# An opening of eight groups of weight columns in a decoder layer on one core, with one load of forget weights and an earlier copy of c

## The chip, the core and the metric

One NeuronCore of a Trainium2 chip runs the whole layer in one launch. The metric is the device time of one execution in microseconds. TensorE (PE in the profile) multiplies into eight PSUM banks; VectorE (DVE), ScalarE (ACT) and GpSimd (POOL) do the rest; SyncE (SP) only issues loads.

## What is computed

One decoder layer on 512 positions of 1024 channels, in float32. Two attention branches read the same modulated input u; one combined projection gives queries, keys and values of both, the forget logits of eight heads and two sets of 1024 gates:

```python
mod = c @ w_ada + b_ada
sh1, sc1, gt1, sh2, sc2, gt2 = jnp.split(mod, 6)
u = x * (1.0 + sc1) + sh1
proj = u @ w_in     # fox q,k,v | forget logits | stick-breaking q,k,v | gates A | gates B
log_f = log_sigmoid(f_a + b_forget)
y_fox = softmax(q k^T / 8 + cumsum(log_f)_t - cumsum(log_f)_s, causal) v
y_sb = stick_breaking(q k^T / 8) v
merged = sigmoid(g_a) * (y_fox @ w_fox_proj) + sigmoid(g_b) * (y_sb @ w_sb_proj)
x = layer_norm(alpha * x + (1 + gt1) * (merged @ w_o))
...                 # then a gated MLP with a causal convolution, and a second layer norm
```

## The kernel before

Every product is made of three in a reduced float32: an operand is split into a high part h (a rounded copy, by ScalarE) and a low part l (the difference, by VectorE), and h x h, l x h and h x l are summed in a PSUM bank. One such product has 128 x 128 weights and 512 positions.

**The opening** (lines 222 to 395) runs over the eight tiles j of 128 input channels. `first_load` (line 250) issues the loads of a tile on SP's queue: the two rows `wa` of w_ada for shift and scale, the row `r` of the first weight columns (`w1`, W1C = 904 columns: 128 for the first pair's queries, 128 for its keys, NG = 5 gate groups of 128 for the stick-breaking branch, and 8 forget columns), and x. Tile 0's row is loaded in two parts, columns 0 to 383 and 384 to 903. The small bias of the forget logits is loaded behind tile 6.

c is spread over all partitions by eight select products into banks 6 and 7 (line 234), among warm-up products (`heat`) that keep TensorE working. For tile 0, `first_acc` (line 272) sums w_ada times c on VectorE straight out of these two banks, half of c at a time; then `first_mod` has ScalarE copy the two banks into `cbc` (line 339), from which all later sums read. `bcols` holds the biases; ScalarE adds 1.0 to some of its columns (line 131). For the other tiles `mod_col` (line 243) makes a sum of 1024 and an addition, once for shift and once for scale.

`first_split` (line 294) has ScalarE copy a row to `wh`; `first_mod` (line 312) makes u of the tile, its high and low part, and the low part of the weights. For tile 0 VectorE makes u's high part itself (line 331) while ScalarE makes the full u. `first_pad` (line 304) makes the rest of tile 0's low part and copies the 8 forget columns to `fw`. `first_mm` (line 363) issues the products of a tile: 7 groups x 3 = 21, each group into a bank of its own (grp[0] to grp[6]), accumulated over the eight tiles. Groups 0 to 4 of a tile come first, then the next tile's `first_mod`, then groups 5 and 6. For tile 0 the high products of groups 0 to 2 come ahead of the rest. At tile 7, `forget_mm` (line 356) puts the eight forget products between groups: they write bank 7, which c had before.

**The stream.** Everything else of the projections is a list of work (`stream`, lines 707 to 816): the other pairs' queries and keys, the values, the remaining gates of the stick-breaking branch (`gb`, groups 5 to 7), and later the gates of the other branch and the output projections. Each piece has a weight load of 512 KB (`add_item`), split by ScalarE and VectorE. `add_ada` puts in a further row of w_ada, which costs VectorE a sum and TensorE nothing.

**The heads.** From line 855 on, sixteen heads run, eight stick-breaking ones first. Each head's scores (`stage_a`), transposes (`stage_b`) and products with the values (`stage_c`) are interleaved with products from the stream: `fill(n)` issues n of them. `FILL` (line 48) has the three amounts for each of the first eight heads and of the last eight. Behind the opening, `gate_after` (lines 840 and 847) takes the sigmoid of the gate banks.

Only SP's order is written by hand; on the other engines a scheduler orders the instructions by their dependencies, held in places by `issue_after`. `paced` makes one instruction wait for another.

Of the kernel before, what the change touches and what calls it, by code (L numbers as in the profile page):

```python
# [8 lines left out]
F32 = mybir.dt.float32  # L9
# [3 lines left out]
ALU = mybir.AluOpType  # L13
# [12 lines left out]
NH = 8  # L26
ALPHA = 2.0 ** 0.25
EPS = 1e-5
NEG = -1.0e30
W1C = 904  # L30
NG = 5
PAIRS = [(1, p) for p in range(4)] + [(0, p) for p in range(4)]
# [14 lines left out]
CUT = 5  # L47
FILL = (15, 18, 18), (11, 11, 11)


@with_exitstack
def layer_kernel(ctx: ExitStack, tc: tile.TileContext, out, xT, x, c8, wa0, wa1, bcol, w1, wct, wv, bf,
                 wp, wo, lncol, lnrow, wup, cwb, wdp):
# [30 lines left out]
    def const(shape, dt, s):  # L84
        return cons.tile(shape, dt, name=s, tag=s)
# [43 lines left out]
    g = G.tensor_copy(crow[0:KT], c8s)  # L129
    for q in (slice(1, 2), slice(3, 6)):  # L130
        S.activation(bcols[:, q, :], bcols[:, q, :], AF.Copy, bias=1.0)
    mska = preset([P, 512], F32, "mska")
# [7 lines left out]
    G.tensor_copy(dg[:, 384:512], ident)  # L140
    bfs = const([NH, 1], F32, "bfs")
    modc = const([P, 4, KT], F32, "modc")
# [82 lines left out]

    fw = early.tile([P, KT, NH], F32, name="fw", tag="fw")
    us = []
    def heat(n):
# [3 lines left out]
    for k in range(KT):  # L232
        o = grp[6 + k // 4][:, k % 4 * P : (k % 4 + 1) * P]
        m = PE.matmul(o, sel[:, k : k + 1].broadcast_to([P, P]), ctop, start=True, stop=True)
    with tc.issue_after(m.ins):
        heat(WARM[1])
# [6 lines left out]
    def mod_col(w, col, wt):  # L243
        mod_sum(w, col, wt, slice(0, D), 0)
        b, o = bcols[:, w, col : col + 1], modc[:, w, col : col + 1]
        return V.tensor_tensor(o, modr[:, w, col, 0:1], b, ALU.add)

    x0 = early.tile([P, 512], F32, name="x0", tag="x0")

    def first_load(j):  # L250
        wa = [early.tile([P, D], F32, name=nm("wa"), tag="wa", bufs=5) for _ in range(2)]
        r = stg.tile([P, 1024], F32, name=nm("raw"), tag="raw", bufs=LOADS)
        xt = z(F32, "xt")
        if j == 0:
            for e in range(2):
                nc.sync.dma_start(wa[e], wa0[j, e])
            nc.sync.dma_start(r[:, 0:384], w1[j][:, 0:384])
            nc.sync.dma_start(x0, xT[j * P : (j + 1) * P, :])
            nc.sync.dma_start(r[:, 384:W1C], w1[j][:, 384:W1C])
        else:  # L260
            nc.sync.dma_start(wa[0], wa0[j, 0])
            if j == 1:
                nc.sync.dma_start(wa[1], wa0[j, 1])
            nc.sync.dma_start(r[:, 0:W1C], w1[j])
            if j > 1:
                nc.sync.dma_start(wa[1], wa0[j, 1])
            nc.sync.dma_start(xt, xT[j * P : (j + 1) * P, :])
            if j == 6:
                nc.sync.dma_start(bfs, bf)
        pend[j] = [wa, xt, r]  # L270

    def first_acc(j):
        wa = pend[j][0]
        if j == 0:
            s = state["chl"]
            for e in range(2):
                for q in range(2):
                    c = slice(q * 512, (q + 1) * 512)
                    with tc.issue_after(s.ins):
                        s = mod_sum(q, j, wa[e], c, e, grp[6 + e])  # L280
                    if e or q:
                        for m in heat(WARM[2] + e * q):
                            paced(m, s)
                    if e and not q:
                        with tc.issue_after(s.ins):
                            s = V.tensor_tensor(bcols[:, 0:2, j], bcols[:, 0:2, j], modr[:, 0:2, j, 0], ALU.add)
            with tc.issue_after(s.ins):
                state["modc"] = V.tensor_tensor(modc[:, 0:2, j], modr[:, 0:2, j, 1], bcols[:, 0:2, j], ALU.add)
        else:
            if j == 1:  # L290
                mod_col(0, j, wa[0])
            state["modc"] = mod_col(1, j, wa[1])

    def first_split(j):
        r = pend[j][2]
        h = stg.tile([P, 1024], F32R, name=nm("wh"), tag="wh", bufs=WBUFS)
        l = stg.tile([P, 1024], F32R, name=nm("wl"), tag="wl", bufs=WBUFS)
        if j:
            hi_of(h[:, 0:W1C], r[:, 0:W1C])
        else:  # L300
            state["h"] = S.activation(h[:, 0:384], r[:, 0:384], AF.Copy)
        pend[j][2:] = [h, l, r]

    def first_pad(j):
        h, l, r = pend[j][2:]
        if j == 0:
            c = slice(384, W1C)
            state["after"] = lo_of(l[:, c], r[:, c], h[:, c])
        f = slice(W1C - NH, W1C)
        hi_of(fw[:, j, :], r[:, f])  # L310

    def first_mod(j):
# [15 lines left out]
        else:  # L328
            h, l, r = pend[j][2:]
            with tc.issue_after(state["modc"].ins):  # L330
                ts = V.tensor_scalar(a, x0, sc, sh, ALU.mult, ALU.add)
            with tc.issue_after(state["h"].ins):
                u = S.activation(xt, x0, AF.Identity, bias=sh, scale=sc)
            c = slice(384, W1C)
            with tc.issue_after(u.ins):
                u = S.activation(h[:, c], r[:, c], AF.Copy)
            for e in range(2):
                with tc.issue_after(u.ins):
                    u = state["u"] = S.activation(cbc[:, e * 512 : (e + 1) * 512], grp[6 + e], AF.Copy)
            with tc.issue_after(ts.ins):  # L340
# [22 lines left out]
    def first_mm(j, gs):  # L363
        ops = [(g, n, m) for g in gs for n, m in enumerate(first_ops(j, g))]
        if j < KT - 1:
            rank = (0, 2, 4, 1, 3, 5)
            ops.sort(key=(lambda o: rank[o[1]] + 3 * (o[0] > 2) if o[0] < 5 else o[1]) if j == 0 else lambda o: o[1])
        for g, n, (w, u) in ops:
            m = PE.matmul(grp[g], w, u, start=j == 0 and n == 0, stop=j == KT - 1 and n == 2)  # L369
        return m  # L370
# [3 lines left out]
    first_split(0)  # L374
    first_acc(0)
    first_mod(0)
    for j in range(KT):
# [11 lines left out]
        if j < KT - 1:  # L389
            first_mm(j, range(5, 7))  # L390
        else:
            forget_mm(first_mm(j, (2, 0, 1)))
            first_mm(j, range(3, 7))

# [261 lines left out]

    sg, ma, wps = {}, {}, {}

    def gate_after(br, j):
# [108 lines left out]
    add_pair(3)  # L768
    add_gate(1, gb.pop(0))
    add_pair(4)  # L770
# [74 lines left out]
    stage_a(1, 0)  # L845
    for j in range(1, NG):
        gate_after(1, j)(grp[2 + j])
# [524 lines left out]
def _pack(inputs):  # L1372
# [16 lines left out]
    def col(kind, n):  # L1389
        if kind in ("sb", "fox"):  # L1390
# [4 lines left out]
    first = [w_in[:, s : s + P] for s in [col("q", 0), col("k", 0)] + [col("sb", j) for j in range(NG)]]  # L1395
    cols = np.concatenate(first + [w_in[:, 1536:1544]], axis=1)
    r["w1"] = c(cols.reshape(KT, P, W1C))
# [3 lines left out]
    r["wct"] = c(np.stack([w_in[:, s : s + P].reshape(KT, P, P).transpose(1, 0, 2).reshape(P, D) for s in starts]))  # L1401
    r["bf"] = c(a["b_forget"].reshape(NH, 1))
    wpj = np.stack([a["w_fox_proj"], a["w_sb_proj"]]).reshape(2, 4, P, 4, 2, P)
# [13 lines left out]

_NAMES = ["xT", "x", "c8", "wa0", "wa1", "bcol", "w1", "wct", "wv", "bf", "wp", "wo", "lncol", "lnrow",
          "wup", "cwb", "wdp"]
# [19 lines left out]
```

## Time and profile before

| | us |
|---|---|
| median of 3 runs | 734.72 |
| lowest, highest | 734.35, 735.94 |
| the profiled execution | 734.0 |
| its span, first to last instruction | 732.2 |
| TensorE busy | 722.6 (99%) |
| VectorE busy | 601.1 (82%) |
| ScalarE busy | 391.7 (53%) |
| GpSimd busy | 88.1 (12%) |

The profile has one execution. In a timeline row stand the start, the time, the engine, the line of the kernel, the operation, what is written and read, its shape, how many instructions are merged into the row, and in brackets how long the engine was idle before and what ended that. Matmuls overlap: the start of the next tells what one costs.

### The profile page before, as it was taken

To read this page: it belongs to the slowest core of one execution; us is meant where nothing else is said; L and a number is where in the kernel's file an instruction comes from. 1 tells how busy PE (TensorE), PEld (TensorE's weight loads), DVE (VectorE), ACT (ScalarE), POOL (GpSimd) and SP (SyncE) were. 2 spreads that over 40 slices of the span, in tenths; PEclk is the share of its full clock that TensorE was granted. 3 is DMA by queue.
4 is the path that set the end of the run, shared out by engine and by line. 5 is a ranking of instruction groups with operands and counts; after the bars stand their busy time and mean duration, and the time that the engine had idled before them with its cause. 6 is when DMAs were issued, how large, how long until landed. Compare 5 with 4: busy or idle time off the path is not lost.

```text
span 732.2 us, 9844 instructions
## 1 busy us (share of the span) xinstructions
PE 722.6 (99%) x3444; PEld 602.3 (82%) x3444; DVE 601.1 (82%) x1041; ACT 391.7 (53%) x684; POOL 88.1 (12%) x142
## 2 busy tenths in 40 slices
PE   8999999999999999999999999999999999999996
PEld 5878888888888888888889888888888888888885
DVE  7978799778898886873697999978887787679996
ACT  5576466686885754442056553444453544347550
POOL 1045224352010000000000001000011010000010
PEclk9999999999999999999999999999999999999999
DMA  9953535423332241632075688577699777646733
GB/s 354 404 208 126 175 116 196 149 88 115 118 116 100 75 170 60 228 124 86 1 259 143 205 250 250 162 249 227 200 349 252 210 239 209 203 161 227 223 89 92
DMA packets 45490, 131.96 MB, mean 180 GB/s; under 512 B 6168, under 2 KB 7200, under 8 KB 45440
## 3 DMA queue, kind: packets, MB, share of 16 engines
q1 hardware_dynamic: 38176, 112.61, 44.6%
q0 software_dynamic: 4224, 10.30, 7.0%
q10 hardware_dynamic: 3040, 8.42, 3.1%
q8 instruction: 27, 0.44, 0.2%
q14 instruction: 23, 0.19, 0.1%
HBM read 118.39 MB, written 12.85 MB: 179 GB/s over the span
## 4 chain that ended last, share of the span: by engine, by line
PE 97%; DMA 1%; DVE 1%; ACT 0%; issue 0%; DVEq 0%
PE ps L152 19%; PE ps L154 19%; PE ps L153 19%; PE ps L1152 5%; PE ps L1153 5%; PE ps L1154 5%; PE ps L369 5%; PE ps L613 3%; PE ps L595 2%; PE ps L521 2%; PE ps L523 2%; PE ps L522 2%; PE ps L944 2%; PE ps L945 2%; PE ps L943 2%; PE ps L547 1%
## 5 line engine op out<-in xcount | busy, mean ns | idle before, releaser
L217 ACT ACTIVATE wh<-raw 128x1024 fp32r<-128x1024 f32 (+1 forms) x105 | 109.1, 1041 | 105.0 <-PE ps L153 47.2
L94 DVE TENSOR_TENSOR wl<-raw,wh 128x1024 fp32r<-128x1024 f32 (+2 forms) x114 | 137.2, 1204 | 30.6 <-ACT wh L217 29.5
L152 PE MATMUL ps<-u2h,wh 128*128 128x512 f32 (+1 forms) x376 | 141.3, 376 | 0.0
L153 PE MATMUL ps<-u2l,wh 128*128 128x512 f32 (+1 forms) x376 | 141.2, 375 | 0.0
L154 PE MATMUL ps<-u2h,wl 128*128 128x512 f32 (+1 forms) x376 | 141.2, 375 | 0.0
L153 PEld LDWEIGHTS ps<-u2l,wh 128*128 128x128 f32 x376 | 70.8, 188 | 12.8
L154 PEld LDWEIGHTS ps<-u2h,wl 128*128 128x128 f32 x376 | 70.8, 188 | 12.8
L152 PEld LDWEIGHTS ps<-u2h,wh 128*128 128x128 f32 x376 | 70.8, 188 | 12.7
L152 PE MATMUL ps<-uh,wh 128*128 128x512 f32 x200 | 79.5, 397 | 0.0
L154 PE MATMUL ps<-uh,wl 128*128 128x512 f32 x200 | 78.1, 391 | 0.0
L153 PE MATMUL ps<-ul,wh 128*128 128x512 f32 x200 | 77.9, 390 | 0.0
L1205 ACT ACTIVATE cv<-ps,cw 128x512 f32<-128x512 f32 x44 | 34.0, 774 | 48.1 <-PE ps L154 40.9
L1206 DVE SCALAR_TENSOR_TENSOR cv<-ps,cw,cv 128x511 f32<-128x511 f32 x44 | 32.8, 746 | 23.0 <-ACT cv L1205 23.0
L154 PEld LDWEIGHTS ps<-uh,wl 128*128 128x128 f32 x200 | 37.5, 188 | 8.3
L153 PEld LDWEIGHTS ps<-ul,wh 128*128 128x128 f32 x200 | 37.6, 188 | 7.4
L152 PEld LDWEIGHTS ps<-uh,wh 128*128 128x128 f32 x200 | 37.5, 188 | 7.4
L240 DVE SCALAR_TENSOR_TENSOR raw<-raw,cbc 128x1024 f32<-128x1024 f32 x32 | 39.6, 1240 | 0.0
L575 POOL TENSOR_TENSOR pt<-pt,om 128x127 f32<-128x127 f32 (+3 forms) x32 | 38.6, 1217 | 1.4 <-DVE om L574 1.3
L181 POOL DMA_DIRECT2D raw<-in_wdp x10 | 8.9, 886 | 244.6 <-DMA raw<-in_wdp 228.1
L1207 DVE SCALAR_TENSOR_TENSOR cv<-ps,cw,cv 128x510 f32<-128x510 f32 x44 | 32.8, 744 | 0.4
L574 DVE TENSOR_TENSOR_SCAN om<-om,dg 128x127 f32<-128x127 f32 (+3 forms) x32 | 28.9, 962 | 3.8 <-ACT om L569 3.8
L1218 ACT ACTIVATE cv<-cv 128x512 f32<-128x512 f32 x21 | 13.3, 631 | 32.0 <-DVE cv L1207 32.0
(246 smaller groups left out, 1551.8 us busy)
## 6 DMA issues: line engine op xcount, KB each, us to landing
raw<-in_wup SPq DMA_DIRECT2D x44, 512.0 KB, 5.0
raw<-in_wa SPq DMA_DIRECT2D x32, 512.0 KB, 3.6
raw<-in_wct SPq DMA_DIRECT2D x25, 512.0 KB, 4.6
raw<-in_wdp SPq DMA_DIRECT2D x20, 512.0 KB, 5.2
wa<-in_wa SPq DMA_DIRECT2D x16, 512.0 KB, 8.7
raw<-in_wdp SPq DMA_DIRECT2D x22, 256.0 KB, 4.7
raw<-t SPq DMA_DIRECT2D x22, 256.0 KB, 4.7
raw<-in_wdp POOLq DMA_DIRECT2D x10, 512.0 KB, 7.7
```

The costliest lines, as they stand in the source:

```text
L94: state["read"] = V.tensor_tensor(o, i, fl(hi), ALU.subtract)
L152: PE.matmul(ps, wh, ah, start=first, stop=False)
L153: PE.matmul(ps, wh, al, start=False, stop=False)
L154: return PE.matmul(ps, wl, ah, start=False, stop=last)
L217: state["hi"] = S.activation(h[:, 0:cols], r[:, 0:cols], AF.Copy)
L240: state["read"] = V.scalar_tensor_tensor(wt[:, c], wt[:, c], 1.0, cbc[:, c] if by is None else by, ALU.mult, ALU.mult, accum_out=o)
L369: m = PE.matmul(grp[g], w, u, start=j == 0 and n == 0, stop=j == KT - 1 and n == 2)
L575: G.tensor_tensor(pt[b][:, s : e - 1], pt[b][:, s : e - 1], om[:, s + 1 : e], ALU.mult)
L1152: PE.matmul(ps, ah, bh, start=first, stop=False, skip_group_check=onto)
L1153: PE.matmul(ps, ah, bl, start=False, stop=False, skip_group_check=onto)
L1154: return PE.matmul(ps, al, bh, start=False, stop=last, skip_group_check=onto)
L1205: tap = S.activation(t, ps, AF.Identity, bias=cw[:, n, 3:4], scale=cw[:, n, 2:3])
```

## The change

W1C becomes 1024 and NG 6: the row of the opening holds six gate groups and no forget columns, and each tile has eight groups, 24 products, into all eight banks. The forget weights come in one load `fwt` of [128, 65] floats, with the bias in its last column, behind tile 6. At tile 7 group 7 is first, its sigmoid is taken at once, and the forget products come behind groups 2 and 3. In the stream the gate behind pair 3 goes (its w_ada row stays), and FILL's first triple is 15, 17, 16.

For tile 0, ScalarE copies bank 7 right behind the select products and bank 6 once VectorE has made its second sum, instead of both behind the weights. VectorE makes u's high part in two halves of 256 positions, and the high products of groups 0 and 1 are issued in halves, first halves first. One product of zeros goes into each of banks 0 and 1 as a warm-up product and opens them, so that the halves can accumulate; four warm-up products among the sums become three. `mod_col` makes one addition for shift and scale together.

```diff
-W1C = 904
-NG = 5
+W1C = 1024
+NG = 6
...
-FILL = (15, 18, 18), (11, 11, 11)
+FILL = (15, 17, 16), (11, 11, 11)
...
-    for q in (slice(1, 2), slice(3, 6)):
-        S.activation(bcols[:, q, :], bcols[:, q, :], AF.Copy, bias=1.0)
...
-    bfs = const([NH, 1], F32, "bfs")
+    fwt = const([P, KT * NH + 1], F32, "fwt")
+    fw = fwt[:, 0 : KT * NH].rearrange("p (k h) -> p k h", h=NH)
+    bfs = fwt[0:NH, KT * NH : KT * NH + 1]
...
         m = PE.matmul(o, sel[:, k : k + 1].broadcast_to([P, P]), ctop, start=True, stop=True)
+    s = S.activation(cbc[:, 512:1024], grp[7], AF.Copy)
+    for q in (slice(1, 2), slice(3, 6)):
+        with tc.issue_after(s.ins):
+            s = S.activation(bcols[:, q, :], bcols[:, q, :], AF.Copy, bias=1.0)
+    state["bcols"] = s
...
-        mod_sum(w, col, wt, slice(0, D), 0)
-        b, o = bcols[:, w, col : col + 1], modc[:, w, col : col + 1]
-        return V.tensor_tensor(o, modr[:, w, col, 0:1], b, ALU.add)
+        s = mod_sum(w, col, wt, slice(0, D), 0)
+        if w:
+            s = V.tensor_tensor(modc[:, 0:2, col], modr[:, 0:2, col, 0], bcols[:, 0:2, col], ALU.add)
+        return s
...
             if j == 6:
-                nc.sync.dma_start(bfs, bf)
+                nc.sync.dma_start(fwt, fwb)
...
                         s = mod_sum(q, j, wa[e], c, e, grp[6 + e])
+                    if q and not e:
+                        with tc.issue_after(state["bcols"].ins):
+                            state["copy"] = S.activation(cbc[:, 0:512], grp[6], AF.Copy)
                     if e or q:
-                        for m in heat(WARM[2] + e * q):
-                            paced(m, s)
+                        m = PE.matmul(grp[q if e else 5], warm[:, 0:P], warm, start=True, stop=not e)
+                        paced(m, s)
...
-            state["h"] = S.activation(h[:, 0:384], r[:, 0:384], AF.Copy)
+            first_acc(0)
+            with tc.issue_after(state["copy"].ins):
+                state["h"] = S.activation(h[:, 0:384], r[:, 0:384], AF.Copy)
...
-        f = slice(W1C - NH, W1C)
-        hi_of(fw[:, j, :], r[:, f])
...
-            with tc.issue_after(state["modc"].ins):
-                ts = V.tensor_scalar(a, x0, sc, sh, ALU.mult, ALU.add)
+            ts = state["modc"]
+            for c in (slice(0, H), slice(H, T)):
+                with tc.issue_after(ts.ins):
+                    ts = V.tensor_scalar(a[:, c], x0[:, c], sc, sh, ALU.mult, ALU.add)
...
-            for e in range(2):
-                with tc.issue_after(u.ins):
-                    u = state["u"] = S.activation(cbc[:, e * 512 : (e + 1) * 512], grp[6 + e], AF.Copy)
+            state["u"] = u
...
-        for g, n, (w, u) in ops:
-            m = PE.matmul(grp[g], w, u, start=j == 0 and n == 0, stop=j == KT - 1 and n == 2)
+        split = 2 if ops[0][0] == 0 and j == 0 else 0
+        for c in (slice(0, H), slice(H, T)):
+            for g, n, (w, u) in ops[0:split]:
+                m = PE.matmul(grp[g][:, c], w, u[:, c], start=False, stop=False)
+        for g, n, (w, u) in ops[split:]:
+            m = PE.matmul(grp[g], w, u, start=j == 0 and n == 0 and g > 1, stop=j == KT - 1 and n == 2)
...
         if j < KT - 1:
-            first_mm(j, range(5, 7))
+            first_mm(j, range(5, 8))
         else:
-            forget_mm(first_mm(j, (2, 0, 1)))
-            first_mm(j, range(3, 7))
+            first_mm(j, (7, 0, 1))
+            sg[(1, NG - 1)] = z(F32, "sg")
+            S.activation(sg[(1, NG - 1)], grp[7], AF.Sigmoid)
+            forget_mm(first_mm(j, (2, 3)))
+            first_mm(j, range(4, 7))
...
     add_pair(3)
-    add_gate(1, gb.pop(0))
+    add_ada()
...
-    for j in range(1, NG):
+    for j in range(1, NG - 1):
         gate_after(1, j)(grp[2 + j])
...
```

## Rows read from the trace of the kernel before

**Rows 1.** Busy us of the engines, share of the span, instructions (page).

```profile
PE 722.6 (99%) x3444; PEld 602.3 (82%) x3444; DVE 601.1 (82%) x1041; ACT 391.7 (53%) x684; POOL 88.1 (12%) x142
```

**Rows 2.** TensorE's waits, whole run: who, for whom, us in total, times, longest.

```profile
PE ps L369 <- DVE uh L331: 0.3, 1, 0.3
PE ps L369 <- ACT uh L317: 0.2, 1, 0.2
```

**Rows 3.** Chain that ended last, 0 to 20 us: start, us, what.

```profile
4.12 7.34 DMA raw<-in_w
...
11.48 0.69 ACT wh L91
...
12.35 0.81 ACT uh L317
```

**Rows 4.** Timeline of TensorE, 0 to 62 us.

```profile
3.30 1.05 PE L234 MATMUL ps<-crow,sel 128*128 128x128 bf16 x8
4.15 1.81 PE L229 MATMUL ps<-warm 128*128 128x512 bf16 x4
...
7.03 0.60 PE L229 MATMUL ps<-warm 128*128 128x512 bf16 x2 [0.29 <-DVE wa L240]
7.93 0.93 PE L369 MATMUL ps<-uh,wh 128*128 128x512 f32 x3 [0.29 <-DVE uh L331]
...
12.34 0.61 PE L369 MATMUL ps<-ul,wh 128*128 128x512 f32 x2
13.20 1.43 PE L369 MATMUL ps<-uh,wh 128*128 128x512 f32 x5 [0.25 <-ACT uh L317]
...
23.06 1.30 PE L369 MATMUL ps<-uh,wh 128*128 128x512 f32 x5
...
42.10 0.39 PE L369 MATMUL ps<-uh,wh 128*128 128x512 f32 x1
...
49.00 0.39 PE L152 MATMUL ps<-uh,wh 128*128 128x512 f32 x1
...
52.30 0.28 PE L546 MATMUL ps<-m,s 128*128 128x256 f32 x1
52.41 0.28 PE L547 MATMUL ps<-m,s 128*128 128x256 f32 x1
```

**Rows 5.** Timeline of all engines, 0 to 20 us.

```profile
5.60 0.69 DVE L240 SCALAR_TENSOR_TENSOR wa<-wa,ps 128x512 f32<-128x512 f32 x1
...
5.72 0.32 ACT L131 ACTIVATE bcols<-bcols 128x8 f32<-128x8 f32 x2 [2.46 <-DMA bcols<-in_bcol]
...
6.23 0.52 ACT L301 ACTIVATE wh<-raw 128x384 fp32r<-128x384 f32 x1 [0.19 <-DMA raw<-in_w]
...
7.01 0.16 DVE L288 TENSOR_TENSOR modc<-modr,bcols 128x2 f32<-128x2 f32 x1
...
7.24 0.55 DVE L331 TENSOR_SCALAR uh<-x,modc 128x512 fp32r<-128x512 f32 x1
7.70 0.55 DVE L94 TENSOR_TENSOR wl<-raw,wh 128x384 fp32r<-128x384 f32 x1
...
8.47 1.06 ACT L339 ACTIVATE cbc<-ps 128x512 f32<-128x512 f32 x2
...
11.48 0.96 ACT L91 ACTIVATE wh<-raw 128x904 fp32r<-128x904 f32 x1 [1.86 <-DMA raw<-in_w]
```

**Rows 6.** DMA issues (KB each, us to landing); windows (last: clock, DMA share, GB/s).

```profile
raw<-in_w SPq DMA_DIRECT2D x7, 452.0 KB, 8.0
...
10.00:11.00 1.00, 1.00 (x7) 0.80 (x6) 1.00 (x3) 0.00 (x0) 0.00 (x0) 1.00 1.02 408
```

**Rows 7.** Timelines of VectorE and TensorE at the second head.

```profile
108.00 0.55 DVE L94 TENSOR_TENSOR ptc<-ps,ptc 128x384 fp32r<-128x384 f32 x1
...
109.64 0.34 PE L613 MATMUL ps<-ptc,vv 128*128 128x256 f32 x2
```

**Rows 8.** Window 50 to 200 us: PE, PEld, DVE, ACT, POOL busy, clock, DMA.

```profile
50.00:200.00 150.00, 150.00 (x749) 127.05 (x748) 125.09 (x190) 103.49 (x190) 54.61 (x79) 1.00 0.40 138
```

More of the change, by code (lines that the diff above doesn't have):

```diff
@@ L47, with layer_kernel @@
 CUT = 5
-FILL = (15, 18, 18), (11, 11, 11)
+FILL = (15, 17, 16), (11, 11, 11)
 @with_exitstack
-def layer_kernel(ctx: ExitStack, tc: tile.TileContext, out, xT, x, c8, wa0, wa1, bcol, w1, wct, wv, bf,
+def layer_kernel(ctx: ExitStack, tc: tile.TileContext, out, xT, x, c8, wa0, wa1, bcol, w1, wct, wv, fwb,
                  wp, wo, lncol, lnrow, wup, cwb, wdp):
@@ L224, in layer_kernel @@
     pend = {}
-    fw = early.tile([P, KT, NH], F32, name="fw", tag="fw")
-    us = []
+    us, sg, ma = [], {}, {}
     def heat(n):
@@ L374, in layer_kernel @@
     first_split(0)
-    first_acc(0)
     first_mod(0)
@@ L655, in gate_rows @@
         yield 0
-    sg, ma, wps = {}, {}, {}
     def gate_after(br, j):
@@ L1395, in _pack @@
     first = [w_in[:, s : s + P] for s in [col("q", 0), col("k", 0)] + [col("sb", j) for j in range(NG)]]
-    cols = np.concatenate(first + [w_in[:, 1536:1544]], axis=1)
+    cols = np.concatenate(first, axis=1)
+    fwb = np.zeros((P, KT * NH + 1), np.float32)
+    fwb[:, 0 : KT * NH] = w_in[:, 1536:1544].reshape(KT, P, NH).transpose(1, 0, 2).reshape(P, KT * NH)
+    fwb[0:NH, KT * NH] = a["b_forget"]
+    r["fwb"] = fwb
     r["w1"] = c(cols.reshape(KT, P, W1C))
@@ L1401, in _pack @@
     r["wct"] = c(np.stack([w_in[:, s : s + P].reshape(KT, P, P).transpose(1, 0, 2).reshape(P, D) for s in starts]))
-    r["bf"] = c(a["b_forget"].reshape(NH, 1))
     wpj = np.stack([a["w_fox_proj"], a["w_sb_proj"]]).reshape(2, 4, P, 4, 2, P)
@@ L1415, in _pack @@
     return r
-_NAMES = ["xT", "x", "c8", "wa0", "wa1", "bcol", "w1", "wct", "wv", "bf", "wp", "wo", "lncol", "lnrow",
+_NAMES = ["xT", "x", "c8", "wa0", "wa1", "bcol", "w1", "wct", "wv", "fwb", "wp", "wo", "lncol", "lnrow",
           "wup", "cwb", "wdp"]
```

## The prediction

> **What bounds the kernel now.** I read the page's busy shares first, then TensorE's waits, the chain of waits of the opening, and last the timelines of the opening and of one attention head. TensorE is busy for 722.6 of 732.2 us [rows 1]. Its list of waits over the whole run has four rows, two of warm-up products and the two shown, and all lie before 13.2 us [rows 2]: behind the opening TensorE waits for nobody, except in the last microseconds, which this change doesn't touch. So a gain can only come out of the first 13 us, out of small losses in the tiles behind them, or out of fewer products; and a loss can only come from a new wait in TensorE's dense part.
>
> The unit of everything below: from 23.06 to 42.10 lie four tiles of 21 products, 84 in 19.04 us, or 0.227 us a product [rows 4].
>
> In the opening the chain runs over tile 1. It goes from tile 1's weight row (landed at 11.46) to ScalarE's copy of it (11.48), to ScalarE's u of tile 1 (12.35 to 13.16) and to that tile's first product at 13.20 [rows 3, 4]. TensorE was free before that: the last two of tile 0's 21 products start at 12.34, so another could have started at 12.34 + 2 x 0.227 = 12.79. That hole of 0.41 us is the first of two facts on which the forecast rests. The second: from 13.20 to 23.06 are tiles 1 and 2, 42 products or 9.53 us at the unit, done in 9.86 [rows 4]: another 0.33 us lost to late u's and slow starts.
>
> **The change part by part.**
>
> *Eight groups instead of seven.* The 24 products of the sixth stick-breaking gate move from the later stream into the opening, 3 to a tile, and FILL drops by 3 for each of eight heads, also 24. TensorE's sum of work stays. What changes is how much of it lies ahead of tile 1: tile 0 now has 24 products, so 3 x 0.227 = 0.68 us of work that was paid for later is done in front of the chain's next link. Whether it is free depends on when tile 1 can start.
>
> *When tile 1 can start.* Tile 1's row grows from 452 to 512 KB [rows 6], and the second part of tile 0's row, ahead of it in SP's queue, from 520 to 640 columns. That is 2 x 120 columns x 128 rows x 4 bytes, 122,880 bytes more in front of tile 1's copy. The DMA is full there, at 408 GB/s [rows 6], so the row lands 0.30 us later. Bounds: 0, if the DMA engines had later transfers in hand at 11.46 anyway and give those up; 0.45, if half as much again presses on it. I take 0.30, since the row shows a full DMA. ScalarE's copy of tile 1 grows from 904 to 1024 columns: 0.96 us for 904 and 0.52 for 384 [rows 5] make 0.85 ns a column, so 0.10 us. Tile 1's first product comes at 13.20 + 0.30 + 0.10 = 13.60.
>
> *Is TensorE busy till then?* Tile 0 ends at 12.79 + 0.68 = 13.47 if its first product doesn't move, earlier if it does. Either way that is ahead of 13.60, and tile 1 starts 0.40 us later with 0.68 us more work done. Net: 0.28 us gained; 0.13 with the late landing, up to 0.58 with none (tile 1 at 13.30, which tile 0 only makes if the halves below bring it forward).
>
> *Tile 0's u and first two products in halves.* VectorE takes 0.55 us for u of tile 0, from 7.24, and the first product starts 0.14 us behind its end, at 7.93 [rows 4, 5]. Half of it, 256 columns, takes between half of that, 0.27, and two thirds of the 0.55 that 384 columns took in the next row, 0.37. So the first product starts near 7.7, some 0.2 us earlier. Two products of 256 columns, each with its own weights, start 0.11 us apart, at 52.30 and 52.41 [rows 4], half of the unit, so four halves cost no more than two wholes. On VectorE the two halves may together take up to 0.2 us more than the whole, and all that is queued behind them (the low parts of the weights' first 384 columns, of u and of the other columns, then tile 1's sums) is late by that; u of tile 1 wants those sums at 12.35 now, and at 12.75 then. The 0.2 us gained in front end ahead of tile 1's start, where TensorE waits anyway. I put the halves at 0; up to 0.2 us gained if tile 1's row isn't late.
>
> *c's banks copied early.* The two copies out of PSUM (1.06 us together) leave ScalarE at 8.47 to 9.53. Behind them ScalarE was idle for 1.86 us till tile 1's row landed [rows 5], so nothing on the chain is gained. In their new place bank 7 is copied behind the select products (done at 4.35), and VectorE first reads that bank at 5.60 [rows 4, 5]: 1.25 us for a copy of 0.58. Bank 6 comes behind the two additions of 1.0 to bcols, which wait for their DMA until 5.72 and end at 6.04; its copy ends near 6.6, that of tile 0's first 384 columns (0.52 us) near 7.1, and ScalarE's next instruction needs what VectorE finishes at 7.2 [rows 5]. So: 0, with 0.1 us of cover; beyond that tile 0 is late by the excess, which is hidden for another 0.14 us.
>
> *One load of forget weights.* Eight copies of 8 columns leave ScalarE, and one load of 33 KB takes the place of one of 32 bytes in SP's queue behind tile 6. At 408 GB/s that is 0.08 us of the DMA where products no longer follow transfers: a tile then is 24 x 0.227 = 5.44 us of TensorE against 1.84 MB, or 4.5 us, of transfers. 0.
>
> *Tiles 2 to 7.* With 5.44 instead of 4.76 us of products a tile, while the weights' copies and low parts grow by 0.1 us each, late u's lose less. Of the 0.33 us lost on tiles 1 and 2 I take 0.1 as gained, between 0 and 0.25.
>
> *The end of the opening.* The forget products use bank 7, which now holds the eighth group, so they wait for its sigmoid on ScalarE. Groups 0 to 3 lie between, 12 products or 2.7 us, against a sigmoid that reads the same 512 columns as a copy of 0.6 us. 0; the first pair's queries and keys get 0.68 us more before they are wanted.
>
> *The heads.* Each of the first eight heads has 48 instead of 51 filling products, 0.68 us less cover, one of the three in front of stage_c. At the second head VectorE ends its last low part at 108.55 and TensorE wants it at 109.64 [rows 7]: 1.09 us to spare, of which 0.23 go. VectorE is busy for 125.1 of the 150 us from 50 to 200 [rows 8]; with one weight split of 1.2 us and 5.4 us of time less that is 86%. 0.
>
> Sum: 0.28 + 0.1, so 0.4 us faster; by the bounds 0.1 to 0.9. The profiled execution took 734.0 us (its span of 732.2 and 1.8 around it); 0.4 less is 733.6. The median of the three runs is 734.72, 0.7 above the profiled one; against it the forecast is 734.3.
>
> **The rivals.**
>
> *Nothing moves* (within 0.1 us). Tile 1's row lands 0.6 us late, because the transfers queued behind it press on the same full DMA. For it: the DMA has nothing to spare. Against: SP's queue puts only 0.12 MB more ahead of it. 734.7.
>
> *The whole opening tightens.* Tile 1's row isn't late, the halves count in full, and of the hole of 0.41 and the 0.33 nearly all goes: 0.9 to 1.2 us, 733.6. For it: rows of 4096 bytes may run better than rows of 3616. Against: the same DMA share.
>
> *Slower: the heads lose their cover.* If VectorE's last low part comes 0.86 us or more later against TensorE than at the second head now, TensorE stands in front of stage_c. One weight split of 1.2 us that slips in front of it does that: 0.35 us a head. In two heads it eats the gain, in all eight it costs 2.8 - 0.4 = 2.4 us. For it: a VectorE at 86%, and an order of splits, sums and low parts that shifts with the stream. Against: VectorE enters the heads with a longer lead, since TensorE's opening is 5 us longer. 735.0 to 737.1, middle 736.
>
> *Slower: the clock.* From 4.15 four warm-up products take 1.81 us, 0.45 each, as at the 1.2 GHz level; at 7.93 three take 0.93 and then 0.227 each, the 2.4 GHz level [rows 4]. The change takes one of two warm-up products away at 7.03. If tile 0 ran at the lower level, 24 x 0.22 us less the 0.13 us of room would cost 5 us; from the third such product on it costs more than the gain. For it: TensorE does a little less before tile 0. Against: it stood idle for 0.3 us in front of 7.93 [rows 2], and the next products were fast. 737 to 739. The Trainium skill, "TensorE: Matmul & The Clock Gate", under "Why this matters for your kernels", has the clock fall back to half when products stop between bursts; the trace agrees as far as the slow first products go, and shows no fall behind them.
>
> **How the numbers follow.** Forecast 0.69, nothing moves 0.13, the whole opening 0.07, heads 0.08, clock 0.03. The range takes the forecast with its bounds, the first two rivals and the light end of the heads, from 734.72 - 1.3 to 734.72 + 0.9: 733.4 to 735.6, the medians' scatter of a few tenths included. About 0.2%, 1.5 us, is what a measurement of this kernel can tell from no change. Faster by more needs the whole opening and luck: 0.06. Slower by more needs most of the heads' price or the clock's: 0.07. Same: 0.87.
>
> **What would show it.** In the timeline of the changed kernel: the first product near 7.7; tile 1's row landed near 11.76 and its first product at 13.6, with 24 products before it and a hole of 0.1 to 0.4 us; no wait of TensorE behind 20 us; the stream's first product 5.0 us later than the 49.0 of now [rows 4]. The forecast is wrong if tile 1 starts by 13.3 (more gain), if it starts behind 13.9 (none), or if TensorE's list of waits gets a row behind 50 us.

## The result, and the profile after

The changed kernel takes 737.90 us in the median of six runs (737.06 to 738.62), the kernel before beside it 734.54 (six runs). The ratio is 1.0043, with an interval of 1.0030 to 1.0056: slower by some 3.2 us. The forecast was 734.3, and its range ended at 735.6. The profiled execution took 738.28 us with a span of 736.5, where that of before had 732.2. (Single executions that were disturbed are left out of all figures below; the profile of c1_tile0_only fell into one and isn't read.)

TensorE's busy time on the page stands against [rows 1]:

```profile
PE 723.8 (98%) x3445; PEld 602.3 (82%) x3445; DVE 599.9 (81%) x1034; ACT 387.2 (53%) x673; POOL 88.1 (12%) x142
```

It is busy for 1.2 us more in a span that is 4.3 us longer. So most of the difference is time in which it isn't busy, and the list of TensorE's waits of the changed kernel says for whom (waiter, line, who is waited for, us in total, times, longest). It answers to [rows 2]:

```profile
PE ps L152 <- ACT wh L217: 1.6, 1, 1.6
PE ps L229 <- DVE warm L107: 1.2, 1, 1.2
PE ps L380 <- DVE uh L342: 0.9, 1, 0.9
PE ps L537 <- DVE wl L94: 0.6, 1, 0.6
PE ps L291 <- DVE wa L245: 0.3, 1, 0.3
PE ps L152 <- DVE cv L1220: 0.2, 1, 0.2
```

Three of them lie behind the opening: one for a stream weight that ScalarE copies late (1.6 us), one for a late low part of a weight (0.6), and a small one far behind (0.2). The prediction had named just that, a row behind 50 us, as the sign that it is wrong.

**The opening** did its 24 products a tile, and gained nothing. TensorE's timeline (start, us, engine, line, what) answers to [rows 4]:

```profile
8.30 0.73 PE L380 MATMUL ps<-uh,wh 128*128 128x256 f32 x4 [0.91 <-DVE uh L342]
...
13.20 0.84 PE L382 MATMUL ps<-ul,wh 128*128 128x512 f32 x3
14.16 1.43 PE L382 MATMUL ps<-uh,wh 128*128 128x512 f32 x5
...
54.53 0.39 PE L152 MATMUL ps<-uh,wh 128*128 128x512 f32 x1
```

Tile 0 has its 24 products, the last three from 13.20, so a further one could have started at 13.20 + 3 x 0.227 = 13.88. Tile 1 starts at 14.16. The stream's first product comes at 54.53, 5.53 us later than at 49.00 in [rows 4]; 24 products more are 5.44 us. The opening's balance in this execution is a loss of 0.09 us. ScalarE's timeline shows why tile 1 is late, against [rows 5]:

```profile
5.90 0.58 ACT L289 ACTIVATE cbc<-ps 128x512 f32<-128x512 f32 x1
6.98 0.52 ACT L312 ACTIVATE wh<-raw 128x384 fp32r<-128x384 f32 x1 [0.51 <-DMA raw<-in_w]
...
12.35 1.06 ACT L91 ACTIVATE wh<-raw 128x1024 fp32r<-128x1024 f32 x1 [3.12 <-DMA raw<-in_w]
13.31 0.80 ACT L326 ACTIVATE uh<-xt,modc 128x512 fp32r<-128x512 f32 x1
```

Tile 1's row landed at 12.32 (in the chain of waits it takes 8.07 us, against 7.34 in [rows 3]). The early copy of c's second bank ends at 6.48 and holds up nobody: behind it ScalarE waits for a DMA. The halves waited for x: VectorE's two halves of u begin at 7.74, behind a wait of 0.60 us for x's transfer.

**The loss** lies for the most part between 132 and 148 us. The timeline of all engines there:

```profile
130.71 1.39 DVE L94 TENSOR_TENSOR m<-ps,m 64x512 fp32r<-64x512 f32 x2 [3.48 <-ACT m L91]
...
132.02 1.21 DVE L245 SCALAR_TENSOR_TENSOR raw<-raw,cbc 128x1024 f32<-128x1024 f32 x1
...
133.16 1.22 DVE L245 SCALAR_TENSOR_TENSOR raw<-raw,cbc 128x1024 f32<-128x1024 f32 x1
133.26 0.33 SPq L174 DMA_DIRECT2D raw<-in_wct  x1
...
136.73 1.06 ACT L217 ACTIVATE wh<-raw 128x1024 fp32r<-128x1024 f32 x1 [0.49 <-DMA raw<-in_wct]
...
137.84 0.50 PE L152 MATMUL ps<-uh,wh 128*128 128x512 f32 x1 [1.59 <-ACT wh L217]
```

Read it from the bottom: TensorE waits 1.59 us for ScalarE's copy; the copy waits for a load of weights (pair 4's keys); SP issues that load only at 133.26. Its issue before that stands at 115.65, so SP's queue stood for 17.6 us, for a buffer: the load goes into the buffer of a row of w_ada, which is free when VectorE has summed that row. That SP stands is nothing new. At the same place in the kernel before it stood for 11.9 us, and from 271 us on for 15.9, without a wait of TensorE; what is new is that here it lasts 5.7 us longer. SP's timelines, first after, then before:

```profile
115.65 0.39 SPq L174 DMA_DIRECT2D raw<-in_wa  x1
133.26 0.33 SPq L174 DMA_DIRECT2D raw<-in_wct  x1
```

```profile
112.41 0.38 SPq L174 DMA_DIRECT2D raw<-in_wct  x1
124.31 0.33 SPq L174 DMA_DIRECT2D raw<-in_wa  x1
```

Two such sums (L245) stand directly behind each other at 132.02 and 133.16, behind the low parts of pair 3's keys (m, 130.71), which themselves wait for TensorE's products. In the kernel before VectorE's timeline has the two sums apart and both ahead of m:

```profile
123.06 1.22 DVE L240 SCALAR_TENSOR_TENSOR raw<-raw,cbc 128x1024 f32<-128x1024 f32 x1
...
125.34 1.22 DVE L240 SCALAR_TENSOR_TENSOR raw<-raw,cbc 128x1024 f32<-128x1024 f32 x1
...
126.48 1.39 DVE L94 TENSOR_TENSOR m<-ps,m 64x512 fp32r<-64x512 f32 x2
```

The edit that did it is the shortest of the diff: behind pair 3 the stream has a bare row of w_ada (`add_ada()`) where a gate with its row stood. Pair 3 ends with such a row already, so two come in succession. A row's sum isn't placed where the row stands in the list. It is held until another item's weights are split (`release()`, lines 189 to 194 of the changed kernel), and pinned behind the last low part given out by then. With a gate between the rows, its weight's split releases the first one. Without it both are given out only behind pair 3's keys and their low parts.

### The profile page after: what moved, and what is told of

It is laid out like the page before. It is cut to its first block, busy times and chain, and to the rows that moved or that the text cites. A ratio compares the mean times of both kernels' runs of the same rounds, so it can differ in the third digit from the quotient of the medians.

```text
span 736.5 us, 9820 instructions
## 1 busy us (share of the span) xinstructions
PE 723.8 (98%) x3445; PEld 602.3 (82%) x3445; DVE 599.9 (81%) x1034; ACT 387.2 (53%) x673; POOL 88.1 (12%) x142
## 4 chain that ended last, share of the span: by engine, by line
PE 89%; DMA 4%; DVE 4%; ACT 2%; issue 0%; DVEq 0%
PE ps L152 17%; PE ps L154 17%; PE ps L153 17%; PE ps L382 5%; PE ps L1167 4%; PE ps L1166 4%; PE ps L1165 4%; PE ps L628 2%; PE ps L610 2%; PE ps L537 2%; PE ps L538 2%; PE ps L957 2%; PE ps L958 2%; PE ps L536 2%; PE ps L956 2%; PE ps L562 1%
## 5 line engine op out<-in xcount | busy, mean ns | idle before, releaser
L217 ACT ACTIVATE wh<-raw 128x1024 fp32r<-128x1024 f32 x104 | 108.0, 1040 | 106.9 <-PE ps L153 40.1
L152 PE MATMUL ps<-uh,wh 128*128 128x512 f32 x192 | 76.5, 398 | 1.6 <-ACT wh L217 1.6
L154 PE MATMUL ps<-uh,wl 128*128 128x512 f32 x192 | 75.1, 391 | 0.0
L153 PE MATMUL ps<-ul,wh 128*128 128x512 f32 x192 | 74.8, 390 | 0.0
L154 PEld LDWEIGHTS ps<-uh,wl 128*128 128x128 f32 x192 | 36.0, 188 | 8.0 <-DVE wl L94 0.2
L153 PEld LDWEIGHTS ps<-ul,wh 128*128 128x128 f32 x192 | 36.1, 188 | 7.1
L245 DVE SCALAR_TENSOR_TENSOR raw<-raw,cbc 128x1024 f32<-128x1024 f32 x32 | 39.4, 1235 | 0.0
```

The source lines that it names most:

```text
L152: PE.matmul(ps, wh, ah, start=first, stop=False)
L153: PE.matmul(ps, wh, al, start=False, stop=False)
L154: return PE.matmul(ps, wl, ah, start=False, stop=last)
L217: state["hi"] = S.activation(h[:, 0:cols], r[:, 0:cols], AF.Copy)
L245: state["read"] = V.scalar_tensor_tensor(wt[:, c], wt[:, c], 1.0, cbc[:, c] if by is None else by, ALU.mult, ALU.mult, accum_out=o)
```

## The experiments

Three theories stood at first. *Queue* (A where letters stand): the bare row of w_ada holds back the loads, and that is the loss. *Cover* (B): the heads have less filling work than they need, as one of the prediction's rivals had it. *Pace* (D): the rounding in `fill` (next run) lets the stream run ahead of its loads. Another cause came up on the way: the place of the forget chain, the steps from the forget logits to their cumulative sum, on ScalarE.

**Fewer fillings in fact.** FILL = (15, 17, 16) changes nothing: `fill(n)` takes groups of three products until n is used up, so 17 and 16 take 18 each, as 18 does. The heads kept their 51 products, and the stream runs 24 products ahead of them instead. This run gives the heads the 48 of the prediction:

```
-FILL = (15, 17, 16), (11, 11, 11)
+FILL = (15, 15, 18), (11, 11, 11)
```

> The changed kernel with FILL 15, 15, 18. fill() counts down by the 3 products of a step, so 17 and 16 issue 18 products each, just as 18 does: the changed kernel still issues 51 a head, and this one the 48 that the change meant. Theory A (queue): in the stream two rows of w_ada now follow each other behind pair 3; VectorE's sums of them come behind the low parts of pair 3's keys, the load of pair 4's key weights waits for the first of these sums, and TensorE waits for these weights. Then nothing changes: a wait of TensorE of 1.5 to 2.5 us at the first product of pair 4's keys, 737 to 738.5. Theory D (pace): the rounding makes the stream run ahead of its loads; then the wait goes, 735.0. Theory B (cover): fewer products beside the heads; then it gets worse, over 738.5.

Measured: 744.06 us (743.61 to 745.92), ratio 1.0132 [1.0118, 1.0146], another 6.2 us above the changed kernel. From its list of waits:

```profile
PE ps L152 <- ACT wh L217: 2.8, 1, 2.8
PE ps L610 <- DVE m L94: 2.1, 1, 2.1
```

And from its windows (us of the window, then busy us of PE, PEld, DVE, ACT, POOL, the granted clock, the DMA's share and GB/s):

```profile
140.00:144.00 4.00, 3.94 (x14) 3.31 (x15) 3.92 (x5) 2.14 (x4) 4.00 (x4) 0.58 0.42 160
...
161.00:165.00 4.00, 4.00 (x15) 3.28 (x14) 4.00 (x5) 4.00 (x10) 3.81 (x7) 0.57 0.02 4
```

So the cover matters in this stream: with 48 products the same wait grows from 1.6 to 2.8 us, another of 2.1 appears at 160 us, and behind each of the two the granted clock falls to about 0.57 of full speed, mostly the 1.2 GHz level, for 4 us, which loses 4 x (1 - 0.575) = 1.7 us each time. Both waits and both slow stretches make 8.3 us; less the 2.2 us of waits that the changed kernel has in their place, that is 6.1, where the two medians differ by 6.2 and the two spans by 5.8. So cover is a cause where it is taken away, against what queue alone expected, and pace, by which the wait had to go, is out. Cover is not what the changed kernel suffers from, since that has its 51. What 48 products would cost without the bare row was not run.

**The bare row taken out of the change.** The row comes later with the rest.

```
     add_pair(3)
-    add_ada()
     add_pair(4)
```

> The changed kernel without the row of w_ada that stands in the gate's place behind pair 3 (all 24 rows are still loaded, each later one a place later). Theory A: the sums stand ahead of pair 3's keys again and TensorE's wait is gone, 3.1 us less than the changed kernel, 734.5 to 735.2: what is left against before is the opening, +0.1. Theories B and D: no difference, 737.5 to 738.

Measured: 735.97 us (734.96 to 737.15), ratio 1.0020 [1.0012, 1.0029], 1.9 us less than the changed kernel instead of 3.1. The waits near 137 and 145 us are gone, as the queue theory has it; 1.2 us short of its figure, there is a new one (TensorE's timeline):

```profile
157.44 1.10 PE L610 MATMUL ps<-ident,pt 128*128 128x128 f32 x6 [0.83 <-ACT pt L585]
```

**The bare row put into the kernel before**, with its seven groups and old opening:

```
     add_pair(3)
-    add_gate(1, gb.pop(0))
+    add_ada()
...
     add_values(0, 0)
+    add_proj(("sb", gb[0]), gate_after(1, gb.pop(0)))
     add_gate(1, gb.pop(0))
```

> The kernel before, with only the stream changed: the gate behind pair 3 moves to behind the second values, and a row of w_ada stands in its place, so that two follow each other. All products and fillings stay. Theory A: 2 to 3.3 us slower than before, 736.5 to 738, with TensorE's wait at pair 4's keys. Theories B and D: as before, 734.5.

Measured: 737.07 us (736.68 to 738.74), ratio 1.0036 [1.0024, 1.0048], with the waits of the changed kernel 5 us earlier:

```profile
PE ps L152 <- ACT wh L217: 1.4, 1, 1.4
...
PE ps L522 <- DVE wl L94: 0.5, 1, 0.5
```

That is most of the change's loss, without any of its opening. It isn't the bare row's price alone. In this run, too, the values come 24 products earlier, and ScalarE has the forget chain (below) ahead of a head's sigmoids, as in the changed kernel:

```profile
141.51 0.61 ACT L425 ACTIVATE fq<-fq 8x512 f32<-8x512 f32 x1
...
150.41 1.28 ACT L569 ACT_TABLE_LOAD   x1
151.70 0.60 ACT L569 ACTIVATE om<-ps 128x512 f32<-128x512 f32 x1
```

Product by product against the kernel before, its profile falls behind by 2.6 us at the late weights (till 142.44) and by 0.15 behind the sigmoids (153.56).

**The row pitch.** Rows of 1024 columns lie 4096 bytes apart in DRAM. This run is a2 with w1 padded to 1032 columns, of which 1024 are loaded.

> As a2_one_row_less, with the rows of w1 in DRAM padded from 1024 to 1032 columns, so that they lie 4128 bytes apart instead of 4096; the same bytes are loaded. Theory C (pitch): tile 0's x landed at 7.7 and tile 1's row 0.85 us later than before because rows 4096 bytes apart load slower; then tile 1's row lands 0.4 to 0.6 us earlier than in a2_one_row_less and the time falls by as much, 734.2. Theory C' (bytes and order): no difference in landing beyond 0.15 us, and the time of a2_one_row_less.

Measured: 736.18 us (734.72 to 738.17), ratio 1.0018 [1.0009, 1.0027]: as a2. Its opening was 1.4 us shorter in the profile (stream's first product at 54.34, in a2 at 55.72), but most of that is the clock, not the pitch: ScalarE's copy of tile 1 began only 0.20 us earlier (12.19 against 12.39), which lies between the two expectations. In a2's execution TensorE waited 0.99 us in front of tile 0, and then ran at the 1.2 GHz level for 3 us; its windows:

```profile
8.00:9.00 1.00, 0.59 (x4) 0.63 (x5) 1.00 (x4) 1.00 (x2) 0.00 (x0) 0.87 1.01 409
9.00:10.00 1.00, 1.00 (x4) 0.84 (x4) 1.00 (x3) 0.28 (x1) 0.00 (x0) 0.50 1.02 418
```

In the changed kernel's execution the wait was 0.91 and the clock held; in a1's it was 1.32, and the clock held as well.

**The forget chain.** What a2 and a3 had left was a wait for sigmoids. ScalarE's timeline of a3 shows what stood in front of them:

```profile
146.50 1.28 ACT L441 ACT_TABLE_LOAD   x1
...
149.06 1.28 ACT L442 ACT_TABLE_LOAD   x1
...
152.97 0.63 ACT L91 ACTIVATE chi<-fq 8x512 fp32r<-8x512 f32 x1 [0.52 <-DVE fq L444]
153.62 1.28 ACT L584 ACT_TABLE_LOAD   x1
154.92 0.60 ACT L584 ACTIVATE om<-ps 128x512 f32<-128x512 f32 x1
```

The forget chain runs Abs, Exp and Ln on ScalarE, two steps on VectorE, and a rounded copy (chi) on ScalarE again. With the way back to the sigmoids it has three loads of ScalarE's tables, of 1.28 us each. The seventh head's scores are done by 151.4, its first sigmoid runs at 154.92. Between them stand a copy of a weight, the chain's rounded copy with its wait for VectorE, and the last of the table loads. The chain is released by a step of the second branch's values, and these come 24 products earlier, since the stream is ahead. In the kernel before it ran behind that head's sigmoids. The Trainium skill, "ScalarE activation tables: per-element evaluation and per-set limits", under "What a function is on this engine", puts functions of different sets one table load of 1283 ns apart; the trace agrees (1.28 us). The run is a3 with the chain pinned there again:

```
-                forget(items[vfi[0]][5])
+                forget(hd[heads[6]]["last"])
```

> The run a3_pad with one edit: the forget chain on ScalarE (Abs, Exp, Ln with their table loads) is put behind the sigmoids of the seventh head instead of behind the values, so it stands behind them as in the kernel before. Theory (the rest of a2's and a3's loss is the wait of 0.8 us that TensorE has for sigmoids standing behind the forget chain): 735.2 to 735.5, no row L610<-ACT pt of 0.8 us. Rival (the wait only moves, or the loss sits in the opening): 735.9 to 736.4.

Measured: 734.40 us (733.41 to 736.61), ratio 0.9996 [0.9987, 1.0006]: 1.8 us below a3, where 0.7 to 1.0 was expected, and level with the kernel before. Product by product, a3's profile falls behind that of c4 at one place only, by 1.27 us from 156.06 on, the wait of 0.83 and the slow starts around it. The rest of the medians' difference is in the executions: seven of a3's twelve ran at a mean granted clock of 0.996 or less, and three of c4's. The medians of the others are 735.10 and 734.24, or 0.9 apart, as the theory has it. Where those seven lost their clock no trace shows.

**Both causes at their root.** In the changed kernel the two entries of the stream are exchanged, so that the gate stays where it stood:

```
     add_pair(3)
-    add_ada()
+    add_gate(1, gb.pop(0))
...
     add_values(0, 0)
-    add_gate(1, gb.pop(0))
+    add_ada()
```

> The changed kernel with two entries of its stream exchanged: the one remaining later gate stays behind the fourth pair, as in the kernel before, and the row of w_ada without a product of its own takes its place behind the second values. Opening and everything else as in the change. Theory (the 3.2 us are the held back loads, by two rows of w_ada behind one another, and the forget chain's new place; the opening costs 0 to 0.5): 734.5 to 735.0, no wait of TensorE for L217 or L585 between 100 and 170 us. Rival (the opening itself loses 1 us or more): 735.5 to 736.2 without those waits. Rival (the two rows stall wherever they stand): above 736.5 with a wait behind the second values, near 165 us.

Measured: 734.51 us (733.85 to 735.60), ratio 0.9997 [0.9989, 1.0006]. This one exchange takes away 3.4 us. In its list of waits nothing is left behind the opening, and ScalarE has the forget chain behind the sigmoids again:

```profile
154.62 0.64 ACT L585 ACTIVATE pt<-ps 128x512 f32<-128x512 f32 x1
155.09 0.61 ACT L440 ACTIVATE fq<-fq 8x512 f32<-8x512 f32 x1
155.72 1.28 ACT L441 ACT_TABLE_LOAD   x1
```

Held against c5, whose opening is the same, the profile of the changed kernel falls behind by 0.14 us up to the stream, then by 1.89 and 2.69 at the two late weights (137.84 and 139.10), 2.87 behind the wait at 145.52, 3.35 behind the forget chain and 3.74 at 468 us, where it waits once for VectorE (cv). That last 0.4 us (0.8 in c8, below) comes in two of the four profiles with the held back loads, not in a1 and b1, and in none without them; how it hangs together with them stays open.

**The forget chain alone**, pinned in the changed kernel with the bare row left in:

> The changed kernel with one edit, the forget chain pinned behind the sigmoids of the seventh head; the two rows of w_ada behind one another stay. Theory (two causes, of which the held back loads stand first: in the changed kernel TensorE has already waited 2.2 us in this stretch when it comes to the sigmoids, so the forget chain is nearly covered): 737.0 to 737.9, the waits for L217 and L94 near 137 and 145 us still there. Rival (the forget chain alone costs its 1.8 us in every stream): 736.0 to 736.3.

Measured: 737.57 us (736.57 to 738.54), ratio 1.0040 [1.0028, 1.0052], with the waits for L217 and L537 as in the changed kernel (1.4 and 0.5 us). The two causes don't add: a TensorE that has stood 2.2 us for loads comes to the sigmoids so much later that only some 0.5 us of the chain still shows.

**The edits of tile 0 alone**, in the kernel before with its seven groups:

> The kernel before with only the edits of tile 0: both copies of c's banks early, u and the first two products in halves, the pacing products as in the change; seven groups, FILL 18, stream untouched. Theory (the edits of tile 0 are worth nothing, since tile 1's row sets the opening's end): 734.4 +- 0.4, the first product 0.1 to 0.3 us earlier than in the kernel before, tile 1's first product unmoved near 13.2, the stream's first product at 49.0 to 49.7. Rival (the longer chain of halves and copies costs the opening up to 1 us, by a late tile 1): 735.0 to 735.5, stream's first product above 49.7.

Measured: 734.42 us (734.03 to 734.97), ratio 0.9995 [0.9987, 1.0004]. No gain is seen there.

**The groups without them**, first in a2:

> The run a2_one_row_less with the edits of tile 0 undone: eight groups and the one load of forget weights alone; copies of c's banks and u of tile 0 as in the kernel before. Theory (the wider rows set the opening): as a2_one_row_less, 735.7 to 736.3, first product near 8.2, tile 1's row landed behind 12. Rival (the halves and early copies brought the loss of the opening): 735.0 to 735.5, first product at 7.9.

Measured: 737.5 us (736.72 to 740.84), ratio 1.0044 [1.0026, 1.0063], above both expectations. The profiled execution took 738.12. It has the forget chain's wait and a stall that no other run has:

```profile
312.45 0.50 PE L154 MATMUL ps<-uh,wh 128*128 128x512 f32 x1 [0.81 <-ACT wh L219]
...
314.60 0.50 PE L156 MATMUL ps<-uh,wl 128*128 128x512 f32 x1 [1.41 <-DVE wl L94]
```

It goes back to a load of w_o that was issued at 301.53 and for which VectorE waited 3.33 us, till 309.05. In a2 that load was issued at 302.63, and VectorE used it at 306.80 without a wait. The stream's first product came at 54.46, so the opening isn't it. To see whether the edits of tile 0 have to do with it, the same edits were undone in c5:

> c5_gate_kept with the edits of tile 0 undone: eight groups and the one load of forget weights alone, in a stream that keeps the gate behind the fourth pair. Theory (the edits of tile 0 decide nothing, since tile 1's row ends the opening; what c2_groups_only lost beside a2_one_row_less was a late load at 309 us that has nothing to do with the opening): as c5, 734.3 to 734.8, stream's first product 54.3 to 54.6, no wait of TensorE near 312 us. Rival (without the early copies and halves eight groups cost 1 to 2 us): 735.5 to 736.5.

Measured: 735.03 us (734.38 to 737.56), ratio 1.0010 [1.0001, 1.0018], without the stall at 312 us. That lies between the two expectations, 0.5 us above c5, and the two intervals overlap. Its profile has the first product at 8.84 and tile 1's at 14.52, 0.44 later than c5's 14.08, and keeps that distance to the end. The 0.44 are tile 1's row: ScalarE's copy of it began at 12.70, in c5 at 12.26. In c2, which is also without the edits, it began at 12.30. So no gain by the edits of tile 0 is shown with eight groups, either. What made c2's load late isn't settled.

**c5 with padded rows**, and then with tile 1's u on VectorE:

> c5_gate_kept with the rows of w1 padded to 1032 columns in DRAM, so that a row of 1024 is still loaded but the pitch is no longer 4096 bytes. Theory (the pitch decides nothing that the end sees; tile 1's row lands near 12.25 as in c5): 734.3 to 734.7, stream's first product 54.2 to 54.6. Rival (the pitch made the transfers of the first 8 us late): tile 1's row at 11.8 to 12.0, stream's first product near 54.1, 734.1.

Measured: 734.17 us (733.51 to 736.59), ratio 0.9998 [0.9990, 1.0006]; ScalarE's copy of tile 1 began at 12.14, the stream's first product came at 54.29. That doesn't decide: without padding the copy began between 12.08 and 12.91 in the seven profiles of eight groups, with it between 11.96 and 12.28 in four.

```
+            if j == 1:
+                with tc.issue_after(state["modc"].ins):
+                    u = state["modc"] = V.tensor_scalar(a, xt, sc, sh, ALU.mult, ALU.add)
+            else:
+                u = S.activation(a, xt, AF.Identity, bias=sh, scale=sc)
-            u = S.activation(a, xt, AF.Identity, bias=sh, scale=sc)
```

> c6_gate_kept_pad with u of tile 1 computed by VectorE in its idle 0.85 us instead of by ScalarE behind its copy of tile 1's weights. Theory (the hole in front of tile 1 is what the chain over tile 1 leaves, and with a shorter chain the three products more per tile fill it as the prediction reckoned): tile 1's first product at 13.6 to 13.75 instead of 14.1, stream's first product near 54.0, 734.0 to 734.3, 0.3 to 0.4 below c6. Rival (VectorE's later low parts or u of tile 2 give it back): tile 1 early, but stream's first product at 54.3 or later and 734.4.

Measured: 733.76 us (733.39 to 735.54), ratio 0.9994 [0.9985, 1.0003], 0.4 below c6 and 0.7 below the median of before beside it. From its timelines of VectorE and TensorE:

```profile
12.71 0.55 DVE L328 TENSOR_SCALAR uh<-xt,modc 128x512 fp32r<-128x512 f32 x1 [0.38 <-DMA xt<-in_xT]
```

```profile
12.80 0.84 PE L386 MATMUL ps<-ul,wh 128*128 128x512 f32 x3
13.48 1.31 PE L386 MATMUL ps<-uh,wh 128*128 128x512 f32 x5
...
54.01 0.39 PE L152 MATMUL ps<-uh,wh 128*128 128x512 f32 x1
```

Tile 1 follows tile 0 without a hole (12.80 + 3 x 0.227 = 13.48), and the stream begins 0.28 us earlier than in c6. The profile keeps that lead till 573 us and has lost it by 575; both spans are 732.1 us. By the median it is the best version of the study, and by less than can be told from no change.

## Why the prediction was wrong

- **What bounds the kernel**: right. Behind the opening TensorE waits for nobody in the kernel before, and the change lost by new waits in its dense part.
- **The step that failed** is the first of the change, "The 24 products of the sixth stick-breaking gate move from the later stream into the opening", with a cost of nothing in the stream. The products moved, but the row of w_ada that the gate had behind it stayed, next to another row, and the prediction followed neither the row nor SP's queue. Only its products were counted. In the runs, VectorE summed the two neighbouring rows late, SP could issue pair 4's key weights only at 133.26, and TensorE waited 1.6 and 0.6 us. The bare row costs 1.9 us by a2 and, with the forget chain that moved by the same 24 products, 3.4 by c5. In the kernel before, the row and the early chain cost 2.6 us (b1).
- **"FILL drops by 3 for each of eight heads"** failed too: nothing drops, and the stream leads by 24 products. The prediction has no term for what is released by a place in the stream. The forget chain runs ahead of the seventh head's sigmoids in every unpinned run in which the gate's products no longer stand ahead of the values (the changed kernel, a1, a2, a3, b1, c2), and behind them where they do (before, c5, c6, c7, c9). a1 is among the first, so the rounding alone isn't it. The early chain costs 1.3 us by the profiles of c4 and a3, and by their medians 1.8, or 0.9 without the executions at a lower clock.
- **The heads at 0, with a VectorE at 86% and 1.09 us to spare [rows 7, 8]**: the step concerned something the change doesn't do, and its size was wrong as well. With 48 products, and the held back loads still there (a1), the kernel loses 6.2 us more. The room at the second head says nothing of the fourth and sixth, where a held back load and a chain on ScalarE stand in front of TensorE. The rival built on it (one weight split that slips, 735.0 to 737.1) has the right sign and falls 0.8 us short. It even names "an order of splits, sums and low parts that shifts with the stream"; but what it has slip, VectorE's last low part ahead of stage_c, isn't what the trace shows. The late sums held back SP's loads.
- **Tile 1's start**: 13.60 was forecast, it came at 14.16 (14.08 in c5). One execution was taken for the kernel, and it was an early one. With the opening unchanged, b1's profile has the row landed at 11.82 instead of 11.46 and tile 1 at 13.55 instead of 13.20. From there to c5, where it landed at 12.24, are 0.42 us, within the bounds of 0 to 0.45. But the profiles scatter by more: ScalarE's copy of the row began at 11.48 and 11.84 with seven groups (before, b1), and between 12.08 and 12.91, 12.35 in the middle, with eight. So the term of 0.30 us by bytes is rather too small, and its size isn't settled by so few executions. Measured against b1's stream start of 49.66, c5's 54.39 would be a gain of 0.7; against 49.00 it is 0.05.
- **First product near 7.7**: 8.30 in the profile, 7.86 to 8.13 in the padded runs, 7.99 to 8.89 in the other unpadded ones with halves. The two halves took 0.73 us, within the 0.2 more than 0.55 that they were allowed, but x landed later than in the kernel before. A late landing was costed for tile 1 alone; whether the wider rows make x late or executions differ isn't shown, since b1, with the rows of before, also waited for x, for 0.29 us.
- **c's banks copied early, the load of forget weights, the end of the opening**: at nothing, and no row contradicts it.
- **The opening's sum**, 0.4 us faster: in the profiles it was nothing, so the rival "nothing moves" described the opening, with the late row that it names; that the transfers behind the row press on it isn't shown. c5's median is level with that of before, too, though its interval (0.9989 to 1.0006) doesn't shut out 0.4 us. In c7, where the chain over tile 1 is shorter, the stream starts 5.01 us behind 49.00, as "5.0" had it, a gain of 0.43 there, with padded rows. That such a gain reaches the end isn't shown: its profile's span is that of c6.
- **The clock**: the rival's 737 to 739 holds the measured time, but not its cause. The clock held in the profiled execution of the change. It fell in a2's opening, for 3 us and a loss of 1.4 us instead of the 5 that were priced, and twice in a1, in the heads, while its 1.32 us in front of tile 0 brought no fall. The level that the prediction read out of the pace of the warm-up products (0.45 us each) isn't what the windows of the kernel before list there, a granted clock of 1.00 from 4 to 8 us; a2's products at 0.50 do have that pace, 0.43. Which holds the rows don't settle.

## What to carry to other kernels

Moving one group out of a planned stream moves three things: its products, the items that were attached to it, and everything released by a position in the stream. Each has to be followed to the queue it ends in; here SP's loads stood 17.6 us, 5.7 longer than before, because two rows that are summed "when convenient" became neighbours. How long a queue stands says little by itself; what shows the loss is the wait of TensorE at its end. A bare number in a list such as FILL isn't a change until the loop that spends it is read. And a gain of 0.3 us that starts from a DMA's landing time needs that landing from more than one execution.

## What the runs showed of the hardware

A single wait of TensorE of 2.1 to 2.8 us in a dense stretch was followed by 4 us at a mean granted clock of 0.57 to 0.58 (a1), waits of 1.4 to 1.6 us were not (b1, the changed kernel). In front of tile 0, 0.99 us were once followed by 3 us at 0.50 (a2); 0.91, 0.93 and even 1.32 were not (the changed kernel, c9, a1). So a stall can cost more than its own length on top, 1.4 us behind one of 0.99 (a2), and whether it does isn't decided by its length alone.
